# Output projections of a two-layer trunk: tiles 3 to 6 in seven block products per pair

## The chip, the cores and the metric

One core of a Trainium2 chip runs the whole kernel. The time is device microseconds of one launch. The engines are TensorE (PE, with its weight loads as PEld), VectorE (DVE), ScalarE (ACT), GpSimd (POOL) and the queue of SyncE (SP), which here only issues DMAs.

## What is computed

Two layers of a hybrid decoder trunk over 16 learned tokens and 512 others, width 1024, all in float32:

```python
def layer(x):
    h = rmsnorm(x)
    u, z, c_q, c_kv, k_rope, z_mla, g_pool, g_mla = split(h @ w_in)
    y_pool = (pool_mix(u) * silu(z)) @ pool_w_up
    y_mla = (mla(c_q, c_kv, k_rope) * silu(z_mla)) @ mla_w_up      # 8 heads, causal
    merged = sigmoid(g_pool) * y_pool + sigmoid(g_mla) * y_mla
    return x + merged @ w_out                                      # the output projection
```

After the second layer the 16 learned tokens are dropped.

## The kernel before

Everything is held transposed: features on the 128 partitions, tokens along the row (528 in layer 0, 512 in layer 1, where the learned tokens are left out after the keys). A product is made in tiles of 128 output features. Each factor is split into a high and a low part that TensorE multiplies exactly (`whi`, `wlo` of the weights; `hh`, `hl`, `th`, `tl` and so on of the activations), and a product is three matmuls: high by high (L188), high by low (L191), low by high (L192), in `mm3`. ScalarE makes a high part by a copy, VectorE the low part by a subtraction (`split`, `wload`).

The function `stream` runs through a list, `plan`, of products (`Gemm`). Weights come in pieces of 512 columns, four of them ahead, by SP's queue into three buffers `raw`. What happens between two products is written out by hand: `up(name)` runs the stream to a product, `fill_now(ns)` runs it for a while, `after(ns, fn)` puts a job behind it. `behind` makes one instruction wait for another by hand. A scheduler then orders each engine's instructions.

A layer ends with: eight tiles `mu` of the attention's up-projection, whose read-out (`ev_mu`) multiplies by the gate `gms`, adds the pooled half `am` on GpSimd (L1049) and splits the sum into `mg`, that is `hh`/`hl`; and then eight tiles `o` of the output projection. A tile `o` is K = 8 chunks of 128 by the tokens: in layer 0 two halves of 264 columns, so 8 x 3 x 2 = 48 matmuls of 264 columns; in layer 1 24 of 512, its last tile in two halves of 256. Its read-out (`ev_o`, L1063) adds the old residual stream, which SP fetched, and stores the result; in layer 0 it then squares the row for the next norm (`square_x`).

Layer 1 already makes its gate product `gp` in seven block products per pair of tiles (`fast`), a scheme of Strassen and Winograd: weights and activations are cut in two along K, outputs in two along features and tokens, and seven products of sums replace eight. The sums of activations are made by `mixed` in halves; the sums of weights are made in DRAM (`wsum`) by copies on SP's queue and adding DMAs on GpSimd's (`weight_sums`), 32 jobs placed 4500 ns apart over the heads of layer 0. A copy waits by `behind` for a matmul some 9 us back, an add for one some 4 us back.

Of the kernel before, what the change touches and what calls it, by code (L numbers as in the profile page):

```python
# [57 lines left out]
WARM = 8  # L58
SPACE = 4500.0

# [12 lines left out]
def trunk(ctx, tc, xT, pos, win, wkr, wqb, wkb, wvb, wgr, wpu, wmu, wout, gains, const, yT):  # L73
# [88 lines left out]
    class Gemm:  # L162
        def __init__(self, name, src, width, evac=None, xs=None, segs=None, body=None, gain=None):
            self.name, self.src, self.width, self.alloc = name, src, width, mmt
            self.evac, self.xs, self.segs, self.body, self.gain = evac, xs, segs, body, gain
            self.spare = False

# [4 lines left out]

    def wload(src, n, gain, spare):
        raw = early.pop(0) if early else fetch(src, n, rawt(), sp)
# [8 lines left out]
        act.activation(hi[:, :n], raw[:, :n], AF.Copy)  # L183
        dve.tensor_sub(lo[:, :n], raw[:, :n], hi[:, :n].bitcast(F32))  # L184
        return hi, lo
# [13 lines left out]

    newest = [None]  # L200
    plan = []
    done = set()

    def stream():
# [3 lines left out]
        def load(i):  # L208
            g_, c = flat[i]
            n = min(512, g_.width - c)  # L210
            return wload(g_.chunk(c, n), n, g_.gain, g_.spare)

# [116 lines left out]

    wsum = [dp.tile([P, 4, 512], F32, name=f"wsum{u}") for u in range(4)]  # L330
    gate = dp.tile([P, 6, SEQ], F32, name="gate")
# [6 lines left out]

    def weight_sums(w):
        def made(u, i):  # L340
            a, b = w[2 * u], w[2 * u + 1]
            d = wsum[u]
            src = {0: (b[:, 0:512], b[:, 512:1024]), 2: (a[:, 0:512], b[:, 0:512]), 1: (a[:, 0:512], d[:, 0, :]),
                   3: (a[:, 512:1024], d[:, 1, :])}
            return d[:, i, :], src[i]

        def copy(d, src):
            behind(sp.dma_start(d, src[0]), earlier(9000))

        def add(d, src):  # L350
            behind(gp.dma_start(d, src[1], accum_op=ALU.add), earlier(4000))

        for u in range(4):
            for fn, i in ((copy, 0), (copy, 2), (add, 0), (copy, 1), (add, 2), (add, 1), (copy, 3), (add, 3)):
                yield lambda fn=fn, u=u, i=i: fn(*made(u, i))

    class Layer:
        def __init__(self, l):
# [10 lines left out]
            self.csq, self.xsq = [None] * 2, [None] * 8  # L369
            self.sq = []  # L370
            self.f, self.tt, self.part = [None] * 8, [None] * 4, {}
            self.st = self.acc = self.inv = self.cinv = self.kraw = self.kp = None
# [226 lines left out]
        def fast(self, name, a, b, u, got):  # L599
            order = (1, 6, 7, 5, 2, 4, 3)  # L600
            s = wsum[u]
            src = {1: a[:, 0:512], 2: a[:, 512:1024], 4: b[:, 512:1024], 5: s[:, 0, :], 6: s[:, 1, :], 7: s[:, 2, :],
# [439 lines left out]
        def ev_mu(self, m):  # L1042
            def ev(ps, a, b):
                if a == self.x0:
                    self.mg[m] = self.hs[m]
                t = tmp()
                dve.scalar_tensor_tensor(out=t[:, :b - a], in0=self.gms[m][:, a:b], scalar=1.0, in1=ps,  # L1047
                                         op0=ALU.add, op1=ALU.mult)
                gp.tensor_add(t[:, :b - a], t[:, :b - a], self.am[m][:, a:b])  # L1049
                split(*self.mg[m], t[:, :b - a], a, b)  # L1050
            return ev

        def ev_o(self, m, nxt):
            def ev(ps, a, b):
# [17 lines left out]
            return ev  # L1072

        def register(self, nxt):
# [72 lines left out]
        def go(self, nxt):  # L1147
# [11 lines left out]
            if l == 0:  # L1159
                for k in range(8):  # L1160
                    self.square_x(k)
            self.norm_sums()
            up("u1")
            for m in range(2):
# [11 lines left out]
            for s, (a, b) in enumerate(FULL):  # L1176
                a0 = max(a, self.x0)
                self.stat(self.acc[:, a0:b], a0, b, C_CQ, self.acc_last)
            up("qn3")
            self.qk_stats()  # L1180
            if l == 0:
                fill_now(2600)
                for i, fn in enumerate(weight_sums([win[1, MT_GP + m] for m in range(8)])):
                    after(SPACE * (i + 1), fn)
            kq = self.prep(0)
            fill_now(2600)
            due[0] = None
# [22 lines left out]
            if not self.last:  # L1210
                for p in range(4):
                    self.meta_out(p)
            up("o7")
            if nxt is not None:
# [78 lines left out]
```

## Time and profile before

| | |
|---|---|
| median of 3 runs | 788.89 us (788.27 to 788.9) |
| the profiled execution's own time | 788.28 us |
| its span, first to last instruction | 786.4 us |
| mean granted TensorE clock | 1.000 |
| busy: TensorE, VectorE, ScalarE, GpSimd | 778.8, 558.8, 427.1, 210.9 us |
| output projection of layer 0 | 357 to 405 us of the span |
| output projection of layer 1 | 739 to 783 us of the span |

In the profile's rows an operation is named by line, engine, kind and `out<-in`; `xN` is how many it merges, a bracket tells how long the engine was idle before it and who ended that. Matmuls overlap in the records, so TensorE's rate is read from start to start, or from the read-outs of neighbouring tiles.

### The profile page before, as it was taken

What the parts mean: (1) busy time and instruction counts of PE and PEld (TensorE: products, weight loads), DVE (VectorE), ACT (ScalarE), POOL (GpSimd) and SP (SyncE); (2) the same over time, 40 slices, a digit from 0 to 9 for tenths busy, and PEclk for the clock granted to TensorE, in tenths of its full rate; (3) what the DMA queues carried; (4) which work ended last, traced back from release to release, by engine and by line L of the source; (5) the groups of instructions that cost most, each with busy time, mean ns of one, the idle gap of its engine ahead of it and who ended that gap; (6) DMA issues with size and microseconds to landing.
All of it is one profiled execution on the core that took longest, in us unless ns stands there. A gap on an engine that the chain in (4) does not pass through costs nothing.

```text
span 786.4 us, 15094 instructions
## 1 busy us (share of the span) xinstructions
PE 778.8 (99%) x5445; PEld 713.4 (91%) x5445; DVE 558.8 (71%) x1229; ACT 427.1 (54%) x974; POOL 210.9 (27%) x275
## 2 busy tenths in 40 slices
PE   9999999999999999999999999999999999999998
PEld 8999899999999999999997898887778999887887
DVE  5848778447788977685355487775897899874932
ACT  8545655635656665643354455556657676654421
POOL 1034504002434342153000145122004323440600
PEclk9999999999999999999999999999999999999999
DMA  6242343434645435647742422435233454462372
GB/s 243 82 101 84 99 120 102 128 106 117 136 122 126 116 90 112 167 103 176 206 141 81 109 81 79 138 97 167 95 111 112 118 153 126 121 202 68 99 231 100
DMA packets 60907, 97.61 MB, mean 124 GB/s; under 512 B 9744, under 2 KB 18320, under 8 KB 60832
## 3 DMA queue, kind: packets, MB, share of 16 engines
q1 hardware_dynamic: 57520, 90.61, 38.8%
q0 software_dynamic: 2304, 4.20, 4.3%
q10 hardware_dynamic: 1008, 1.84, 0.7%
q8 instruction: 43, 0.70, 0.4%
q14 instruction: 32, 0.26, 0.1%
HBM read 88.64 MB, written 14.23 MB: 131 GB/s over the span
## 4 chain that ended last, share of the span: by engine, by line
PE 91%; DVE 4%; DMA 2%; issue 1%; ACT 1%; ACTq 0%; DVEq 0%
PE mm L188 27%; PE mm L192 27%; PE mm L191 26%; PE mm L944 2%; PE S L191 2%; PE S L192 2%; PE S L188 1%; DVE wlo L184 1%; PE o L950 1%; PE o L949 1%; PE S L498 1%; PE mm L400 1%; DMA xb<-xT 1%; DMA raw<-win 1%; DVE hl L296 0%
## 5 line engine op out<-in xcount | busy, mean ns | idle before, releaser
L188 PE MATMUL mm<-hh,whi 128*128 128x264 f32 (+2 forms) x1080 | 333.9, 311 | 0.1
L191 PE MATMUL mm<-hl,whi 128*128 128x264 f32 (+2 forms) x1080 | 332.5, 309 | 0.4 <-DVE hl L296 0.4
L192 PE MATMUL mm<-hh,wlo 128*128 128x264 f32 (+2 forms) x1080 | 332.1, 310 | 0.4 <-DVE wlo L184 0.4
L184 DVE TENSOR_TENSOR wlo<-raw,whi 128x512 fp32r<-128x512 f32 (+2 forms) x263 | 197.7, 756 | 108.8 <-ACT whi L183 105.3
L183 ACT ACTIVATE whi<-raw 128x512 fp32r<-128x512 f32 (+2 forms) x263 | 157.8, 603 | 179.3 <-PE mm L191 114.6
L188 PEld LDWEIGHTS mm<-hh,whi 128*128 128x128 f32 x1080 | 202.9, 188 | 11.8 <-ACT racc L958 0.5
L191 PEld LDWEIGHTS mm<-hl,whi 128*128 128x128 f32 x1080 | 203.3, 188 | 11.1 <-DVE hl L296 0.9
L192 PEld LDWEIGHTS mm<-hh,wlo 128*128 128x128 f32 x1080 | 202.5, 188 | 10.5 <-DVE wlo L184 1.1
L700 POOL TENSOR_TENSOR racc<-racc,tmp 128x264 f32<-128x264 f32 (+1 forms) x15 | 14.2, 950 | 144.2 <-ACT tmp L699 119.8
L192 PE MATMUL mm<-cq,wlo 128*128 128x264 f32 (+2 forms) x140 | 43.5, 313 | 0.6 <-DVE wlo L184 0.6
L188 PE MATMUL mm<-cq,whi 128*128 128x264 f32 (+2 forms) x140 | 44.0, 314 | 0.0
L191 PE MATMUL mm<-cq,whi 128*128 128x264 f32 (+2 forms) x140 | 43.4, 311 | 0.0
L848 POOL TENSOR_TENSOR tmp<-kp,bc 64x528 f32<-64x528 f32 x16 | 23.7, 1484 | 68.5 <-PE mm L815 44.4
L1049 POOL TENSOR_TENSOR tmp<-tmp,xb 128x264 f32<-128x264 f32 (+1 forms) x24 | 27.2, 1155 | 50.4 <-DVE tmp L1047 38.9
L877 DVE CUSTOM_DVE_ANT_0 S<-S,maskw,nqs 128x288 f32<-128x288 f32 (+4 forms) x80 | 38.3, 497 | 3.0 <-PE S L192 2.8
L922 POOL TENSOR_TENSOR pm<-pa,rs 128x16 f32<-128x16 f32 x32 | 10.9, 340 | 96.7 <-DVE rs L917 88.6
L188 PE MATMUL mm<-u,whi 128*128 128x264 f32 (+1 forms) x108 | 35.2, 326 | 0.1
L296 DVE TENSOR_TENSOR tl<-mm,th 128x512 fp32r<-128x512 f32 (+1 forms) x64 | 29.4, 481 | 7.7 <-ACT th L295 6.5
L192 PE MATMUL mm<-u,wlo 128*128 128x264 f32 (+1 forms) x108 | 34.7, 322 | 0.0
L924 POOL TENSOR_TENSOR cq<-cq,rs 128x384 f32<-128x384 f32 (+1 forms) x32 | 32.8, 1024 | 0.0
L191 PE MATMUL mm<-kn,whi 128*128 128x264 f32 (+1 forms) x96 | 30.6, 320 | 0.0
L188 PE MATMUL mm<-q,whi 128*128 128x264 f32 (+1 forms) x96 | 29.9, 323 | 0.6 <-ACT q L295 0.4
(309 smaller groups left out, 1472.3 us busy)
## 6 DMA issues: line engine op xcount, KB each, us to landing
raw<-win SPq DMA_DIRECT2D x139, 256.0 KB, 2.7
raw<-wout SPq DMA_DIRECT2D x32, 256.0 KB, 3.3
bc<-kdr SPq DMA_DIRECT2D x16, 264.0 KB, 4.1
raw<-wpu SPq DMA_DIRECT2D x16, 256.0 KB, 2.8
wsum<-win SPq DMA_DIRECT2D x16, 256.0 KB, 3.3
raw<-wmu SPq DMA_DIRECT2D x16, 256.0 KB, 2.8
raw<-wsum SPq DMA_DIRECT2D x16, 256.0 KB, 3.2
raw<-wqb SPq DMA_DIRECT2D x12, 256.0 KB, 2.6
```

Source lines behind the costliest of these rows:

```text
L183: act.activation(hi[:, :n], raw[:, :n], AF.Copy)
L184: dve.tensor_sub(lo[:, :n], raw[:, :n], hi[:, :n].bitcast(F32))
L188: first = pe.matmul(out, wh, xh, start=start, stop=False, skip_group_check=more)
L191: pe.matmul(out, wh, xl, start=False, stop=False, skip_group_check=more)
L192: newest[0] = pe.matmul(out, wl, xh, start=False, stop=stop, skip_group_check=more)
L296: dve.tensor_sub(lo[:, a:b], src, hi[:, a:b].bitcast(F32))
L700: self.acc_last = gp.tensor_add(self.acc[:, a:b], self.acc[:, a:b], t[:, :b - a])
L848: gp.tensor_mul(kf[r0:r0 + 64, :], self.kp[r0:r0 + 64, :], bc[r0:r0 + 64, :])
L877: dve.tensor_tensor_reduce(out=sv, in0=sv, in1=mask, scale=nqs[:, i, h:h + 1], scalar=3e38, op0=ALU.add, op1=ALU.min, accum_out=bia[:, c:c ...
L924: gp.tensor_mul(pt[i][:, NM:], pt[i][:, NM:], rs[:, i:i + 1].to_broadcast([P, n - NM]))
L944: pe.transpose(tr[:, P * (i - j):P * (i - j + 1)], pt[i][:, NM + P * j:NM + P * (j + 1)], ident)
L1049: gp.tensor_add(t[:, :b - a], t[:, :b - a], self.am[m][:, a:b])
```

## The change

Of the eight output tiles, 0, 1, 2 and 7 stay as they were. Tiles 3 and 4, and 5 and 6, are made as pairs in seven block products each (`out_pairs`), in both layers: p = 1, 2 and 3 use the activations as they are, p = 4 to 7 the differences that `blend` makes. A product is 4 chunks x 3 = 12 matmuls of half the tokens (264 or 256 columns).

- `blend(k)`, for the four chunk pairs, stands between the `mu` tiles and the first products, while tiles 0 to 2 run: four subtractions on VectorE, in place in `gms`, and three splits. Its first subtraction waits by `behind` for a matmul of the tile in progress.
- `ev_mu` therefore leaves its sum in `gms` in place of a buffer `tmp`.
- Sums of output weights are made in DRAM like those of `gp`: 16 jobs per layer, in the heads. In layer 0 they come first, 3500 ns apart; 22 of the 32 old jobs follow 4000 ns apart, and the other 10 run at the start of layer 1. Layer 1's own 16 are 4500 ns apart in its heads.
- Each product needs its own 512 columns of weights, so weights come for every 12 matmuls of half width. Every second piece uses the slots `kh`/`kl` as raw buffers (`more`).
- The residual rows of tiles 3 to 6 are fetched into `xb` by GpSimd's queue (`residual`), the results are added there and stored by the same queue (`finish`).
- `square_x` of tiles 0 to 6 is made behind the pairs.

```diff
-SPACE = 4500.0
+OUT = (3, 4, 5, 6)
...
+            if g_.more and c % 1024 == 512:
+                return wload(g_.chunk(c, n), n, g_.gain, True, slot(("kh", "kl")[c // 1024 % 2], bufs=2))
...
-                t = tmp()
-                dve.scalar_tensor_tensor(out=t[:, :b - a], in0=self.gms[m][:, a:b], scalar=1.0, in1=ps,
-                                         op0=ALU.add, op1=ALU.mult)
-                gp.tensor_add(t[:, :b - a], t[:, :b - a], self.am[m][:, a:b])
-                split(*self.mg[m], t[:, :b - a], a, b)
+                t = self.gms[m][:, a:b]
+                dve.scalar_tensor_tensor(out=t, in0=t, scalar=1.0, in1=ps, op0=ALU.add, op1=ALU.mult)
+                self.sums[m] = gp.tensor_add(t, t, self.am[m][:, a:b])
+                split(*self.mg[m], t, a, b)
...
-                if b == T:
+                if m == 7:
                     nxt.square_x(m)
...
+        def blend(self, k):
+            a, c = self.x0, T
+            b = (a + c) // 2
+            n = b - a
+            u, w = self.gms[k], self.gms[k + 4]
...
+            behind(dve.tensor_sub(w[:, b:c], u[:, b:c], w[:, b:c]), newest[0])
+            dve.tensor_sub(u[:, b:c], u[:, a:b], u[:, b:c])
+            dve.tensor_sub(u[:, a:b], u[:, a:b], w[:, b:c])
+            dve.tensor_sub(w[:, a:b], w[:, a:b], u[:, a:b])
+            th, tl = slot(f"cq{8 + k}", F32R), slot(f"u{k}", F32R)
+            t3h, t3l, t4h, t4l = (t[:, :n] for t in self.half[4 * k:4 * k + 4])
+            split(th, tl, u[:, a:c], a, c)
+            for h_, l_, v in ((t3h, t3l, w[:, b:c]), (t4h, t4l, w[:, a:b])):
+                split(h_, l_, v, 0, n)
...
+        def residual(self, m):
+            gp.dma_start(xb[:, m, self.x0:T], scr[:, m, :] if self.last else xT[:, m, :])
+
+        def out_pairs(self, nxt):
+            order = [(p, u) for p, u in ((1, 0), (1, 1), (2, 0), (2, 1))] + [(p, u) for u in range(2) for p in (6, 7, 5, 4, 3)]
...
+            def finish(m, s, v):
+                x = xb[:, m, s[0]:s[1]]
+                dve.scalar_tensor_tensor(out=x, in0=v, scalar=0.5, in1=x, op0=ALU.mult, op1=ALU.add)
+                if self.last:
+                    gp.dma_start(yT[:, m, s[0] - NM:s[1] - NM], x)
+                    return
...
+                if p == 1:
+                    act.activation(d, ps, AF.Copy)
+                elif p == 2:
+                    finish(m0, A, ps)
+                elif p == 6:
+                    dve.tensor_sub(d, d, ps)
+                elif p == 7:
+                    dve.tensor_sub(v, ps, d)
+                elif p == 5:
+                    dve.tensor_sub(v, v, ps)
+                    finish(m1, B, v)
...
-            for m in range(8):
+            for m in (0, 1, 2, 7):
+                if m == 7:
+                    self.out_pairs(nxt)
                 add(f"o{m}", wout[l, m], D, evac=self.ev_o(m, nxt), xs=mg,
...
+            if l == 0:
+                jobs.extend(weight_sums("gp", [win[1, MT_GP + m] for m in range(8)]))
+                for i, fn in enumerate(weight_sums(0, [wout[0, m] for m in OUT])):
+                    after(3500 * (i + 1), fn)
+                for i in range(22):
+                    after(16 * 3500 + 4000 * (i + 1), jobs.pop(0))
...
+            if l == 1:
+                for i, fn in enumerate(weight_sums(1, [wout[1, m] for m in OUT])):
+                    after(4500 * (i + 1), fn)
...
+            up("mu7")
+            for m in OUT:
+                self.residual(m)
+            for k in range(4):
+                fill_now(2600)
+                self.blend(k)
             up("o7")
```

How the instructions stand, at the places that matter. First VectorE in layer 0, from the low part of the last gated sum (`hl`) on. Before, only weight splits (L184) and read-outs of tiles (L1063) follow:

```order
L296 TENSOR_TENSOR hl_21_143<-tmp_5205,hh_20_142 128x264
L184 TENSOR_TENSOR wlo_5287<-raw_5284,whi_5286 128x512
L1063 SCALAR_TENSOR_TENSOR xb<-mm_5216,tmp_5261 128x264
L1063 SCALAR_TENSOR_TENSOR xb<-mm_5217,tmp_5277 128x264
L184 TENSOR_TENSOR wlo_5319<-raw_5316,whi_5318 128x512
L184 TENSOR_TENSOR wlo_5360<-raw_5357,whi_5359 128x512
```

Now the four subtractions of `blend` (L1086 to L1089, on the slots `cq`) and the low parts of the differences (L299 into `sq` and `u`) stand among them; read-outs are L1066:

```order
L299 TENSOR_TENSOR hl_21_147<-cq_881_4842,hh_20_146 128x264 x2
L1086 TENSOR_TENSOR cq_825_4512<-cq_734_4040,cq_825_4512 128x264
L184 TENSOR_TENSOR wlo_5324<-raw_5321,whi_5323 128x512
L1087 TENSOR_TENSOR cq_734_4040<-cq_734_4040 128x264
L299 TENSOR_TENSOR sq_5245<-cq_825_4512,sq_5244 128x264
L1088 TENSOR_TENSOR cq_734_4040<-cq_734_4040,cq_825_4512 128x264
L1066 SCALAR_TENSOR_TENSOR xb<-mm_5218,tmp_5289 128x264
L1089 TENSOR_TENSOR cq_825_4512<-cq_825_4512,cq_734_4040 128x264
L1066 SCALAR_TENSOR_TENSOR xb<-mm_5219,tmp_5305 128x264
L1086 TENSOR_TENSOR cq_842_4623<-cq_760_4165,cq_842_4623 128x264
L299 TENSOR_TENSOR u_950_5264<-cq_734_4040,cq_949_5263 128x528
```

From there to the low part of the fourth difference stand 29 operations of 264 columns, 4 of 528 and 6 weight splits.

TensorE in layer 1, where tile 2 before was followed by tile 3 (bank `mm_9911`) in one piece:

```order
L192 MATMUL mm_9870<-hh_20_142,wlo_9867 128x512
L188 MATMUL mm_9911<-hh_6_128,whi_9885 128x512
L191 MATMUL mm_9911<-hl_7_129,whi_9885 128x512
L192 MATMUL mm_9911<-hh_6_128,wlo_9886 128x512
L188 MATMUL mm_9911<-hh_8_130,whi_9885 128x512
```

Now, after tile 2 and the products p = 1 and 2 of the first pair (bank `S_10071`), the first product on a difference (bank `S_10153`, weights `wlo_10130`, difference parts `cq` and `u`) begins, and breaks off after three chunks for the next ones:

```order
L192 MATMUL S_10071<-hh_20_146,wlo_10089 128x256
L192 MATMUL S_10153<-cq_1965_9929,wlo_10130 128x256
L188 MATMUL S_10153<-cq_1972_9970,whi_10129 128x256
L191 MATMUL S_10153<-u_1973_9971,whi_10129 128x256
L192 MATMUL S_10153<-cq_1972_9970,wlo_10130 128x256
L188 MATMUL S_10153<-cq_1982_10017,whi_10129 128x256
L191 MATMUL S_10153<-u_1983_10018,whi_10129 128x256
L192 MATMUL S_10153<-cq_1982_10017,wlo_10130 128x256
L188 MATMUL mm_10173<-sq_9910,whi_10149 128x256
L191 MATMUL mm_10173<-sq_9911,whi_10149 128x256
L188 MATMUL mm_10193<-cq_1965_9929,whi_10169 128x256
```

The widths went from 512 to 256 columns, and each group of 12 matmuls has weights of its own. On VectorE of layer 1, `wlo_10130` has 18 operations of 256 columns and 11 of 512 (itself counted) between it and the last `hl`, and the second pair's first weights, `wlo_10234`, 9 and 6 more.

Last, GpSimd in layer 0. Before, an add of the gated sums is followed by the next, with a job of the weight sums (L351) here and there:

```order
L1049 TENSOR_TENSOR tmp_5120<-tmp_5120,xb 128x264
L1049 TENSOR_TENSOR tmp_5145<-tmp_5145,xb 128x264
L351 DMA wsum_126<-win 128x512
L1049 TENSOR_TENSOR tmp_5163<-tmp_5163,xb 128x264
L1049 TENSOR_TENSOR tmp_5188<-tmp_5188,xb 128x264
```

Now the fetches of residual rows (L1098) stand between the last adds (L1052):

```order
L1052 TENSOR_TENSOR cq_825_4512<-cq_825_4512,xb 128x264
L1098 DMA xb<-xT 128x528
L1052 TENSOR_TENSOR cq_825_4512<-cq_825_4512,xb 128x264
L354 DMA wsumgp_125<-wsumgp_125 128x512
L1098 DMA xb<-xT 128x528
L1052 TENSOR_TENSOR cq_842_4623<-cq_842_4623,xb 128x264 x2
```

Four such fetches stand among the adds of each layer.

More of the change, by code (lines that the diff above doesn't have):

```diff
@@ L165, in __init__ @@
             self.evac, self.xs, self.segs, self.body, self.gain = evac, xs, segs, body, gain
-            self.spare = False
+            self.spare = self.more = False
         def chunk(self, c, n):
@@ L171, in trunk, with wload @@
     loads = [0]
-    def wload(src, n, gain, spare):
-        raw = early.pop(0) if early else fetch(src, n, rawt(), sp)
+    def wload(src, n, gain, spare, buf=None):
+        raw = early.pop(0) if early else fetch(src, n, buf or rawt(), sp)
         loads[0] += 1
@@ L200, in trunk @@
     newest = [None]
+    jobs = []
     plan = []
@@ L328, in trunk @@
     kdr = [dp.tile([H, T], F32, name=f"kdr{l}") for l in range(DEPTH)]
-    wsum = [dp.tile([P, 4, 512], F32, name=f"wsum{u}") for u in range(4)]
+    wsum = {n: [dp.tile([P, 4, 512], F32, name=f"wsum{n}{u}") for u in range(k)] for n, k in (("gp", 4), (0, 2), (1, 2))}
     gate = dp.tile([P, 6, SEQ], F32, name="gate")
@@ L351, in add @@
             behind(gp.dma_start(d, src[1], accum_op=ALU.add), earlier(4000))
-        for u in range(4):
+        for u in range(len(w) // 2):
             for fn, i in ((copy, 0), (copy, 2), (add, 0), (copy, 1), (add, 2), (add, 1), (copy, 3), (add, 3)):
@@ L370, in __init__ @@
             self.sq = []
+            self.sums = [None] * 8
             self.f, self.tt, self.part = [None] * 8, [None] * 4, {}
@@ L1162, in go @@
             self.norm_sums()
+            if l == 1:
+                for i in range(len(jobs)):
+                    after(4000 * (i + 1), jobs.pop(0))
             up("u1")
@@ L1182, in go @@
                 fill_now(2600)
-                for i, fn in enumerate(weight_sums([win[1, MT_GP + m] for m in range(8)])):
-                    after(SPACE * (i + 1), fn)
             kq = self.prep(0)
+            if l == 1:
+                for i, fn in enumerate(weight_sums(1, [wout[1, m] for m in OUT])):
+                    after(4500 * (i + 1), fn)
             fill_now(2600)
@@ L1212, in go @@
                     self.meta_out(p)
+            up("mu7")
+            for m in OUT:
+                self.residual(m)
+            for k in range(4):
+                fill_now(2600)
+                self.blend(k)
             up("o7")
```

56 lines of the change are left out of this document (53 added, 3 removed).

## The prediction

> **What bounds the kernel now.** I read the page first (shares and the chain), then TensorE's waits, then busy time by stretch, and last the timelines of the two output projections.
>
> ```profile
> PE 778.8 (99%) x5445; PEld 713.4 (91%) x5445; DVE 558.8 (71%) x1229; ACT 427.1 (54%) x974; POOL 210.9 (27%) x275
> PE 91%; DVE 4%; DMA 2%; issue 1%; ACT 1%; ACTq 0%; DVEq 0%
> PE wps L137 <- DVE na L817: 1.1, 1, 1.1
> PE mm L192 <- DVE wlo L184: 1.0, 2, 0.6
> 361.50:380.00 18.50, 18.50 (x153) 18.50 (x152) 7.60 (x14) 5.53 (x9) 0.82 (x1) 1.00 0.89 239
> 380.00:405.00 25.00, 25.00 (x206) 25.00 (x205) 11.55 (x21) 11.08 (x19) 0.00 (x0) 1.00 0.59 170
> 747.00:766.00 19.00, 19.00 (x84) 15.43 (x83) 7.63 (x12) 4.42 (x7) 0.00 (x0) 1.00 0.73 233
> 555.00:573.00 18.00, 17.15 (x75) 13.12 (x74) 17.37 (x37) 11.05 (x21) 1.52 (x1) 1.00 0.28 88
> ```
>
> TensorE is busy 99% of the span and 91% of the chain; its longest waits are about 1 us each in total. In the stretches of the output projections (the first three windows; columns: stretch, sum, then busy time and count for PE, PEld, DVE, ACT, POOL, then clock, DMA share, GB/s) it is never idle and its clock is full, while VectorE is busy 7.6 of 18.5 us and 7.6 of 19. So a matmul that is left out there is time saved, as long as its operands come no later. The fourth window is the warning: where VectorE is full (17.37 of 18 us), TensorE loses 0.85 us of 18.
>
> **What goes.** A pair of output tiles is now seven block products instead of eight. VectorE's read-outs of finished tiles give TensorE's rate:
>
> ```profile
> 369.24 0.43 DVE L1063 SCALAR_TENSOR_TENSOR xb<-mm,tmp 128x264 f32<-128x264 f32 x1 [0.46 <-PE mm L192]
> 381.03 0.43 DVE L1063 SCALAR_TENSOR_TENSOR xb<-mm,tmp 128x264 f32<-128x264 f32 x1 [1.06 <-PE mm L192]
> 386.93 0.43 DVE L1063 SCALAR_TENSOR_TENSOR xb<-mm,tmp 128x264 f32<-128x264 f32 x1 [1.06 <-PE mm L192]
> 760.94 0.69 DVE L1063 SCALAR_TENSOR_TENSOR tmp<-mm,tmp 128x512 f32<-128x512 f32 x1 [1.65 <-PE mm L192]
> 766.49 0.69 DVE L1063 SCALAR_TENSOR_TENSOR tmp<-mm,tmp 128x512 f32<-128x512 f32 x1 [1.65 <-PE mm L192]
> 781.84 0.42 DVE L1063 SCALAR_TENSOR_TENSOR tmp<-mm,tmp 128x256 f32<-128x256 f32 x1 [3.57 <-PE mm L192]
> 783.26 0.42 DVE L1063 SCALAR_TENSOR_TENSOR tmp<-mm,tmp 128x256 f32<-128x256 f32 x1 [0.99 <-PE mm L192]
> ```
>
> In layer 0 a tile is 48 matmuls of 264 columns: 386.93 - 381.03 = 5.90 us, 0.1229 us each. A pair goes from 96 to 84, two pairs save 24 x 0.1229 = 2.95 us. In layer 1 a tile is 24 matmuls of 512 columns: 5.55 us, 0.2313 each; the last half of the last tile shows 12 of 256 columns in 1.42 us, 0.1183 each. A pair goes from 48 x 0.2313 = 11.10 to 84 x 0.1183 = 9.94 us, two pairs save 2.32. Together 5.27 us. So a matmul costs about 5.5 ns beyond its columns (2 x 118.3 - 231.3), which layer 1 pays 36 times more per pair. The Trainium skill (TensorE: Matmul & The Clock Gate, "Wait — 56ns, not 53.3ns?") gives columns / 2.4 GHz plus about 2.5 ns, that is 112.5, 215.7 and 109.2 ns; by it the saving would be, as an estimate, 5.06 us instead of 5.27. The rows decide, and they say that the split into halves is dearer and the columns are slower than on that page.
>
> **What is added, and where it lies.** VectorE makes four subtractions and three low parts (one of full width, two of a half) for each of four chunks, between the last low part of the gated sums and the first product that needs a difference. These rows give its rate, by start to start of neighbours:
>
> ```profile
> 353.29 0.42 DVE L296 TENSOR_TENSOR hl<-tmp,hh 128x264 fp32r<-128x264 f32 x1
> 353.63 0.42 DVE L1047 SCALAR_TENSOR_TENSOR tmp<-cq,mm 128x264 f32<-128x264 f32 x1
> 569.37 0.67 DVE L184 TENSOR_TENSOR wlo<-raw,whi 128x512 fp32r<-128x512 f32 x1
> 569.97 0.41 DVE L583 TENSOR_TENSOR cq<-cq,cq 128x256 f32<-128x256 f32 x1
> 570.31 0.41 DVE L584 TENSOR_TENSOR cq<-cq 128x256 f32<-128x256 f32 x1
> 360.98 0.43 DVE L296 TENSOR_TENSOR hl<-tmp,hh 128x264 fp32r<-128x264 f32 x1 [0.20 <-ACT hh L295]
> 746.01 0.68 DVE L296 TENSOR_TENSOR hl<-tmp,hh 128x512 fp32r<-128x512 f32 x1
> ```
>
> 0.34 us for 264 columns (353.29 to 353.63), 0.60 for 512 (569.37 to 569.97), 0.34 for 256 (569.97 to 570.31); 0.62 for 528 is estimated from the slope between them.
>
> *Layer 0.* VectorE's new order has, from the last hl (ends 361.4) to the low part of the fourth difference (u), 29 operations of 264, 4 of 528 and 6 weight splits: 9.9 + 2.5 + 3.6 = 16.0, so 377.4. Tile 1 was read at 369.24, so tile 0 began two tiles earlier, at 357.4; the first product on a difference wants its fourth chunk after 144 + 24 + 9 = 177 matmuls, at 357.4 + 21.8 = 379.2. Slack 1.8 us: cost 0. If the last hl comes 3.4 us late (the third rival) tile 0 itself, which wants it after 40 matmuls (362.3), waits 2.5. Ends 0 and 2.5; I take 0.3, near the lower, since VectorE's row supports it.
>
> *Layer 1.* The last hl ended at 746.7; two weight splits more now stand ahead of it (the ones loaded early into kh and kl), 2 x 0.60: 747.9. Tile 1 ended two tiles before 760.94, at 749.84, so tile 0 began at 738.7 and wants that hl after 40 x 0.2313, at 748.0: no wait. From there to the split of the weights of the first product on a difference (wlo_10130 in the order) stand 18 operations of 256 and 11 of 0.60: 6.1 + 6.6 = 12.7, so 760.6. TensorE wants it after tile 2 and 38 half-wide matmuls: 749.84 + 5.55 + 4.5 = 759.9. It waits 0.7. The next tight place is the second pair's split (wlo_10234): 9 of 256 and 6 of 0.60 more, 3.1 + 3.6, so 767.3, against 749.84 + 5.55 + 88 x 0.1183 = 765.8: 1.5 late in all, and after that a pair of products has 7 x 0.60 + 10 x 0.34 = 7.6 us of VectorE work for 9.9 of TensorE, so the lag shrinks. I take 1.5; ends 0 (VectorE reaches the stage earlier, since sums in place wait for no free tmp) and 3.9.
>
> *Queues.* The residual rows of tiles 3 to 6 are fetched, and their results stored, through GpSimd's queue: four issues among the last adds of each layer.
>
> ```profile
> L351 POOL DMA_DIRECT2D wsum<-win x8 | 6.7, 839 | 56.7 <-PE mm L192 56.7
> L1049 POOL TENSOR_TENSOR tmp<-tmp,xb 128x264 f32<-128x264 f32 x16 | 14.9, 951 | 16.1 <-ACT whi L183 11.5 <-DVE tmp L1047 4.5
> 727.06 4.70 POOL L1049 TENSOR_TENSOR tmp<-tmp,xb 128x512 f32<-128x512 f32 x3 [28.75 <-DVE tmp L1047]
> 729.43 2.88 DVE L184 TENSOR_TENSOR wlo<-raw,whi 128x512 fp32r<-128x512 f32 x2
> 734.26 3.32 POOL L1049 TENSOR_TENSOR tmp<-tmp,xb 128x512 f32<-128x512 f32 x2 [2.49 <-DVE tmp L1047]
> 740.67 4.26 POOL L1049 TENSOR_TENSOR tmp<-tmp,xb 128x512 f32<-128x512 f32 x3 [3.10 <-DVE tmp L1047]
> raw<-wout SPq DMA_DIRECT2D x32, 256.0 KB, 3.3
> wsum<-wsum POOLq DMA_DIRECT2D x8, 256.0 KB, 5.8
> 778.30 5.74 SPq L1067 DMA_DIRECT2D yT<-tmp  x3
> ```
>
> An issue is 0.84 us, four are 3.4. GpSimd idled 4.5 us between its adds in layer 0 and 2.49 + 3.10 = 5.6 in layer 1, waiting for VectorE: that hides them. Each layer's heads get 8 copies on SP's queue and 8 adding DMAs on GpSimd's (5.8 us to landing) for its own output weights; of the 32 old jobs 22 stay in layer 0 and 10 move to the first products of layer 1. SP's loads and GpSimd's window sums and scaling of the probabilities stand behind them. Layer 0 carried 32 such jobs over its heads before with TensorE running on; for layer 1, which had none, no row prices it. Bounds: -0.3 (another order alone) and +1.5 (two landings of 5.8 us of which a quarter shows); I take 0.5. Weights now come every 1.42 us instead of 2.78: 256 KB per 1.42 us is 185 GB/s, under the 239 that the window at 361.5 moved without a wait. The tail is as before: tile 7 stays last, with its two halves and SP's stores; the last GpSimd store is due some 4 us of matmuls earlier.
>
> *Sum*, against the profiled execution's own time (788.28 us; its span is 786.4, so 1.9 lie around it; the median of three runs is 788.89): 788.28 - 5.27 + 0.3 + 1.5 + 0.5 = 785.3. A measurement of this kernel can tell about 0.2%, 1.6 us, from no change.
>
> **Rivals.**
> 1. *All of it arrives.* The sums in place let VectorE run ahead, both layers have slack: 788.28 - 5.27 = 783.0. For it: 7.6 of 19 us busy on VectorE. Against: the 12.7 us counted above leave no slack in layer 1.
> 2. *The gain goes back as small waits.* Each low part needs ScalarE's high part first. If each of the 12 splits of a layer holds VectorE for 0.2 us (the row at 360.98 shows such a 0.20), layer 0 is 2.4 - 1.8 = 0.6 late and layer 1 1.5 + 2.4 = 3.9: 788.28 - 5.27 + 0.6 + 3.9 + 0.5 = 788.0, no change. For it: the window at 555, TensorE losing time where VectorE is full. Against: there only 0.85 us in 18.
> 3. *Slower: GpSimd's queue delays the last sums.* If the four issues don't fall into GpSimd's idle time but push the last adds by 3.4 us, the last hl moves with them, tile 0 waits for it in both layers (2.5 and 3.3), and in layer 1 VectorE's list starts later still behind TensorE's (1.5 as before); differences that then run beside an add slow down, as the two splits at 729.43 did (1.44 us each beside adds, 0.67 alone), 0.5: 788.28 - 5.27 + 2.5 + 3.3 + 1.5 + 0.5 + 0.5 = 791.3, slower. It decides once less than 1 us of the idle is left to fill. For it: the adds are in order behind the issues. Against: GpSimd's idle (4.5, 5.6) was for VectorE, whose products in place now come earlier. The Trainium skill (SBUF — State Buffer, "Who interferes with whom") says that a VectorE operation with two SBUF inputs and a GpSimd operation that reads SBUF block each other for a whole instruction; the trace agrees (1.44 against 0.67).
>
> **How the numbers follow.** Forecast 0.5 (784 to 786.6), rival 1 0.15, rival 2 0.2, rival 3 0.15. Time: 785.3. The range leaves out rival 3 and the very best of rival 1: 783.2 to 788.6. Faster: forecast and rival 1, 0.65; same: rival 2, 0.2; slower: 0.15.
>
> **What would show it.** Right: 48 more matmuls (5493), 84 per pair; read-outs of tiles 0 to 2 still 5.90 and 5.55 apart; the last hl of layer 1 near 748 less what layer 0 gained; TensorE waiting for wlo or u by about 1.5 us in layer 1 and hardly in layer 0. Wrong: waits of TensorE on hl in tile 0 (rival 3); waits of over 3 us in the products (rival 2); a chain that passes through SP's loads there; or heads of layer 1 longer by over 1.5 us.

## The result

The changed kernel took 795.01 us (median of 4 runs, 794.38 to 796.69) against 788.65 before: ratio 1.0084, 95% interval 1.0067 to 1.0102, so 6.4 us slower where 3 us faster was forecast. Its profiled execution took 794.64 us, with a span of 792.8. Three executions among all the runs below took far longer (832.23 us in e5, 934.34 and 1941.56 in e15), and the ratios leave them out.

From the page of the changed kernel, busy time of the engines and the software DMA queue (GpSimd's; packets, MB, share of the DMA engines):

```profile
PE 778.1 (98%) x5493; PEld 713.7 (90%) x5493; DVE 601.0 (76%) x1321; ACT 443.6 (56%) x1015; POOL 238.5 (30%) x315
q0 software_dynamic: 6016, 12.62, 9.8%
```

The same queue before:

```profile
q0 software_dynamic: 2304, 4.20, 4.3%
```

The 48 matmuls more are there (5493). To see what TensorE lost, I took the start of each matmul to the start of the next, less the median of its width (0.122 us for 264 columns, 0.232 for 512, 0.118 for 256), and summed what is over, in us, by stretch of one profiled execution:

| | heads of layer 0 and before (0-355) | its output projection (355-416) | 416-438 | start of layer 1 (438-484) | 484-575 | heads of layer 1 (575-720) | its output projection (720-end) | sum |
|---|---|---|---|---|---|---|---|---|
| before | 17.1 | 0.8 | 1.4 | 1.6 | 4.7 | 6.8 | 0.3 | 32.6 |
| changed | 17.0 | 1.1 | 1.4 | 6.8 | 3.6 | 8.4 | 5.7 | 44.2 |

11.6 us more are lost, 5.27 of matmul time are saved: 6.3, the difference of the two profiled executions (794.64 - 788.28 = 6.36). The loss lies in three places: the start of layer 1 (5.2), layer 1's output projection (5.4), layer 1's heads (1.6); from 484 to 575 us 1.1 less is lost.

**Start of layer 1.** TensorE's waits from 436 to 486 us in the changed kernel (total, times, longest); before it had none there:

```profile
PE mm L188 <- ACT whi L183: 1.4, 1, 1.4
PE mm L188 <- DVE u L545: 1.0, 2, 0.8
PE mm L192 <- DVE wlo L184: 0.7, 2, 0.5
```

The first hangs on a load, as ScalarE's row shows: it stood idle until the weights had landed.

```profile
447.83 1.09 ACT L183 ACTIVATE whi<-raw 128x512 fp32r<-128x512 f32 x2 [6.71 <-DMA raw<-win]
```

The other two stand behind VectorE's work on late data (`wlo`, and the read-out `u`) and weren't traced to their ends. Two windows of the changed kernel (the last two columns are DMA share and GB/s):

```profile
444.00:448.00 4.00, 3.10 (x25) 2.90 (x23) 0.00 (x0) 0.17 (x1) 0.00 (x0) 1.00 1.00 164
448.00:452.00 4.00, 3.27 (x24) 3.06 (x25) 1.88 (x4) 2.68 (x5) 1.77 (x2) 1.00 0.98 231
```

Its loads of the small weights (KB, median us to landing):

```profile
raw<-wkb SPq DMA_DIRECT2D x4, 128.0 KB, 5.7
raw<-wkr SPq DMA_DIRECT2D x1, 128.0 KB, 6.0
```

The same two windows before:

```profile
444.00:448.00 4.00, 4.00 (x23) 3.43 (x22) 0.00 (x0) 0.49 (x2) 1.29 (x1) 1.00 0.65 119
448.00:452.00 4.00, 4.00 (x35) 4.00 (x34) 1.87 (x3) 1.97 (x5) 0.00 (x0) 1.00 0.71 226
```

And the same loads before:

```profile
raw<-wkb SPq DMA_DIRECT2D x4, 128.0 KB, 2.2
raw<-wkr SPq DMA_DIRECT2D x1, 128.0 KB, 2.3
```

The DMA engines are full (1.00 and 0.98, against 0.65 and 0.71) at 164 and 231 GB/s against 119 and 226, and a load of the small weights lands after 5.7 to 6.0 us where 2.2 was enough. GpSimd in the changed kernel shows the second half of it:

```profile
448.08 0.88 POOL L354 DMA_DIRECT2D wsumgp<-wsumgp  x1 [5.52 <-DMA wsumgp<-win]
456.62 0.70 POOL L179 TENSOR_TENSOR raw<-raw,gn 128x256 f32<-128x256 f32 x1 [4.21 <-DMA raw<-wkb]
466.90 0.82 POOL L354 DMA_DIRECT2D wsumgp<-win  x1 [2.38 <-PE mm L192]
```

An adding DMA stands 5.52 us at the head of GpSimd's queue until its copy has landed, another 2.38 us for a matmul; the scaling of the weights (L179) comes at 456.6 where it came at 452.6, although layer 1 began 2.9 us earlier, and what GpSimd owes to the keys behind it is later too.

**Layer 1's output projection.** TensorE's longest wait there in the changed kernel:

```profile
PE mm L191 <- DVE hl L299: 2.0, 1, 2.0
```

VectorE's timeline ahead of it (start, us, what):

```profile
742.96 1.78 DVE L299 TENSOR_TENSOR hl<-cq,hh 128x512 fp32r<-128x512 f32 x1
744.66 0.68 DVE L1051 SCALAR_TENSOR_TENSOR cq<-cq,mm 128x512 f32<-128x512 f32 x1
745.26 0.68 DVE L184 TENSOR_TENSOR wlo<-kh,whi 128x512 fp32r<-128x512 f32 x1
745.87 1.78 DVE L299 TENSOR_TENSOR hl<-cq,hh 128x512 fp32r<-128x512 f32 x1
747.57 0.67 DVE L1051 SCALAR_TENSOR_TENSOR cq<-cq,mm 128x512 f32<-128x512 f32 x1
748.16 0.68 DVE L184 TENSOR_TENSOR wlo<-kl,whi 128x512 fp32r<-128x512 f32 x1
748.77 1.75 DVE L299 TENSOR_TENSOR hl<-cq,hh 128x512 fp32r<-128x512 f32 x1
...
751.04 0.68 DVE L299 TENSOR_TENSOR hl<-cq,hh 128x512 fp32r<-128x512 f32 x1
```

GpSimd's, where the bracket tells the idle time before and what ended it:

```profile
742.52 1.67 POOL L1052 TENSOR_TENSOR cq<-cq,xb 128x512 f32<-128x512 f32 x1 [1.90 <-DVE cq L1051]
744.55 0.56 POOL L1098 DMA_DIRECT2D xb<-scr  x1 [0.36 <-POOL cq L1052]
745.43 1.67 POOL L1052 TENSOR_TENSOR cq<-cq,xb 128x512 f32<-128x512 f32 x1 [0.32 <-DVE cq L1051]
748.32 1.64 POOL L1052 TENSOR_TENSOR cq<-cq,xb 128x512 f32<-128x512 f32 x1 [1.22 <-DVE cq L1051]
```

VectorE is never idle here and goes round in a loop of 2.9 us per tile: product (L1051), a weight split, a low part. Each low part takes 1.78 us in place of 0.68; each of the slow ones lies beside the add that the product just released. Before, the last three products stood in a row. And the order within the loop has changed; the low parts of the sixth and seventh chunk on VectorE, in the order of the program:

```
L299 TENSOR_TENSOR hl_19_145<-cq_1887_9611,hh_18_144 128x512
L1051 SCALAR_TENSOR_TENSOR cq_1907_9681<-cq_1907_9681,mm_9858 128x512
L184 TENSOR_TENSOR wlo_10110<-kl_10107,whi_10109 128x512
L299 TENSOR_TENSOR hl_17_143<-cq_1903_9655,hh_16_142 128x512
```

hl_19 (the seventh chunk) now stands ahead of hl_17 (the sixth), which comes last but one and ends at 750.5. TensorE takes hl_17 first, 28 matmuls behind the start of tile 0 at 741.72, so at 748.2: it waits 2.2 us. What that wait sets off is seen in the windows behind it (PEclk is the last column but two):

```profile
750.50:752.00 1.50, 1.44 (x6) 1.16 (x7) 1.50 (x5) 0.65 (x2) 0.00 (x0) 0.92 0.62 175
752.00:755.00 3.00, 3.00 (x9) 2.33 (x8) 3.00 (x10) 0.97 (x2) 0.00 (x0) 0.50 0.69 201
755.00:757.00 2.00, 2.00 (x10) 1.65 (x9) 1.93 (x5) 1.27 (x3) 0.00 (x0) 0.96 0.03 12
```

For 3.4 us (751.75 to 755.16) the granted clock is 0.50: a 512-column matmul then starts every 0.427 us, not 0.232, and that is 1.6 us more.

### The profile page after: what moved, and what is told of

It reads as the page before. It is cut to its first block, busy times and chain, and to the rows that moved or that the text cites. A ratio compares the mean times of both kernels' runs of the same rounds, so it can differ in the third digit from the quotient of the medians.

```text
span 792.8 us, 15386 instructions
## 1 busy us (share of the span) xinstructions
PE 778.1 (98%) x5493; PEld 713.7 (90%) x5493; DVE 601.0 (76%) x1321; ACT 443.6 (56%) x1015; POOL 238.5 (30%) x315
## 5 line engine op out<-in xcount | busy, mean ns | idle before, releaser
L188 PE MATMUL mm<-hh,whi 128*128 128x264 f32 (+2 forms) x1000 | 308.7, 311 | 2.9 <-ACT whi L183 2.8
L191 PE MATMUL mm<-hl,whi 128*128 128x264 f32 (+2 forms) x1000 | 306.9, 308 | 2.3 <-DVE hl L299 2.3
L192 PE MATMUL mm<-hh,wlo 128*128 128x264 f32 (+2 forms) x1000 | 306.4, 309 | 1.0 <-DVE wlo L184 1.0
L184 DVE TENSOR_TENSOR wlo<-raw,whi 128x512 fp32r<-128x512 f32 (+2 forms) x261 | 195.3, 752 | 100.0 <-ACT whi L183 93.6
L188 PEld LDWEIGHTS mm<-hh,whi 128*128 128x128 f32 x1000 | 188.2, 189 | 14.0 <-ACT whi L183 3.5
L191 PEld LDWEIGHTS mm<-hl,whi 128*128 128x128 f32 x1000 | 188.7, 189 | 12.0 <-DVE hl L299 3.2
L192 PEld LDWEIGHTS mm<-hh,wlo 128*128 128x128 f32 x1000 | 187.8, 189 | 10.4 <-DVE wlo L184 2.1
L1052 POOL TENSOR_TENSOR cq<-cq,xb 128x264 f32<-128x264 f32 (+1 forms) x24 | 28.6, 1220 | 46.8 <-DVE cq L1051 46.6
L299 DVE TENSOR_TENSOR tl<-mm,th 128x512 fp32r<-128x512 f32 (+1 forms) x64 | 29.4, 480 | 7.0 <-ACT th L298 6.0
L354 POOL DMA_DIRECT2D wsum<-wout x8 | 6.8, 848 | 87.8 <-PE mm L192 82.2
L192 PEld LDWEIGHTS mm<-cq,wlo 128*128 128x128 f32 x156 | 29.4, 188 | 2.6 <-DVE wlo L184 1.1
L928 POOL TENSOR_TENSOR cq<-cq,rs 128x384 f32<-128x384 f32 (+1 forms) x32 | 31.6, 989 | 0.0
L888 ACT ACTIVATE cq<-S,bia 128x400 f32<-128x400 f32 (+2 forms) x48 | 24.5, 515 | 12.1 <-DVE bia L916 7.9
```

Source lines behind the costliest of these rows:

```text
L188: first = pe.matmul(out, wh, xh, start=start, stop=False, skip_group_check=more)
L191: pe.matmul(out, wh, xl, start=False, stop=False, skip_group_check=more)
L192: newest[0] = pe.matmul(out, wl, xh, start=False, stop=stop, skip_group_check=more)
L299: dve.tensor_sub(lo[:, a:b], src, hi[:, a:b].bitcast(F32))
L888: act.activation(pv, sv, AF.Exp, scale=-1.0, bias=bia[:, i:i + 1], accum_out=rs[:, c:c + 1])
L928: gp.tensor_mul(pt[i][:, NM:], pt[i][:, NM:], rs[:, i:i + 1].to_broadcast([P, n - NM]))
```

## The experiments

Three theories of the loss were set against the rival on record. A: the ten weight-sum jobs moved to the start of layer 1 delay the weights there (against it stands B: a job costs the same wherever it lies). C: VectorE's order in layer 1 makes tile 0 wait, and the clock drop follows. D (from the second set on): layer 1's own sixteen jobs cost in its heads. The rival is the prediction's third, GpSimd's residual fetches. Every time below stands beside runs of the kernel before on the same chip (788.1 to 788.5), and the ratio is to these; the changed kernel's is 1.0084.

**e1, all 48 jobs in layer 0's heads.**

```diff
-                    after(3500 * (i + 1), fn)
-                for i in range(22):
-                    after(16 * 3500 + 4000 * (i + 1), jobs.pop(0))
+                    after(3000 * (i + 1), fn)
+                for i in range(32):
+                    after(16 * 3000 + 3000 * (i + 1), jobs.pop(0))
```

> All 48 weight-sum jobs of layer 0 run in its heads, 3000 ns apart; none is left for the start of layer 1. Theory A (the ten jobs that were moved to layer 1's first products fill the DMA engines there, and the weight loads land late): the 5 us that TensorE lost between 440 and 483 us go, unless the denser jobs cost something in layer 0's heads: 790 to 791 us against 795.0. Theory B (a job costs the same wherever it lies, by its issue on the queues and its bytes): 795, with the loss moved to 190 to 345 us.

788.22 us, ratio 1.0001 (0.9988 to 1.0014): 6.5 us less than the changed kernel by the ratios, a little more than the 5 expected. The loss from 438 to 484 us fell from 6.8 to 2.4, and the denser jobs cost layer 0's heads nothing (16.4 against 17.0). The output projection of layer 1 kept its 5.6.

**e2, the ten late jobs left out.**

```diff
-            s = wsum["gp"][u]
+            s = wsum["gp"][u % 2]
...
-                for i in range(len(jobs)):
-                    after(4000 * (i + 1), jobs.pop(0))
+                jobs.clear()
```

> The ten late weight-sum jobs are left out altogether (the second half of the gp pairs uses the weights of the first half, so that part of the result is not computed). It prices the ten jobs at the start of layer 1 by themselves. Theory A: 790 us against 795.0, with weight loads from 440 to 483 us landing after some 2.3 us again instead of 5.7 to 6.0. Theory B, or a cause in the pairs of layer 0 that shows only later: 794 to 795.

788.41 us, 1.0007 (0.9999 to 1.0016), with 2.2 lost from 438 to 484. So the ten cost their price by lying at the start of layer 1; in the heads of layer 0 they were free.

**e3, the product in tmp.**

```diff
-                t = self.gms[m][:, a:b]
-                dve.scalar_tensor_tensor(out=t, in0=t, scalar=1.0, in1=ps, op0=ALU.add, op1=ALU.mult)
-                self.sums[m] = gp.tensor_add(t, t, self.am[m][:, a:b])
+                t, v = self.gms[m][:, a:b], tmp()[:, :b - a]
+                dve.scalar_tensor_tensor(out=v, in0=t, scalar=1.0, in1=ps, op0=ALU.add, op1=ALU.mult)
+                self.sums[m] = gp.tensor_add(t, v, self.am[m][:, a:b])
```

> The gated product of the attention's up-projection goes to a buffer tmp again and only the sum is left in gms, which puts VectorE's last products and low parts of layer 1 back into the order of the tiles (hl of tile 5 before that of tile 6). Theory C (sums in place let the scheduler take tile 6 before tile 5 on VectorE; TensorE waits 2.2 us for tile 5's low part in output tile 0, and the clock drop that follows costs 1.6 more): 791 to 792.5 us against 795.0, the wait at 748 us gone or under 1 us. Rival 3 of the prediction (GpSimd's residual fetches among the adds hold the sums): 795, the wait still there.

793.24 us, 1.0060 (1.0044 to 1.0076): 1.9 us less, where 2.5 to 4 were expected. The profile has the mechanism. VectorE:

```profile
743.72 1.27 DVE L1051 SCALAR_TENSOR_TENSOR tmp<-cq,mm 128x512 f32<-128x512 f32 x2
...
747.95 2.51 DVE L299 TENSOR_TENSOR hl<-cq,hh 128x512 fp32r<-128x512 f32 x2
...
750.98 0.68 DVE L299 TENSOR_TENSOR hl<-cq,hh 128x512 fp32r<-128x512 f32 x1
```

Windows over the wait and behind it:

```profile
748.00:751.00 3.00, 2.20 (x10) 1.48 (x9) 3.00 (x5) 1.81 (x4) 1.78 (x2) 1.00 0.90 268
751.00:756.00 5.00, 5.00 (x23) 4.08 (x22) 5.00 (x14) 2.40 (x5) 0.00 (x0) 1.00 0.87 281
```

In the program the order is back (the low part of the sixth chunk before the seventh's), the wait is 0.97 us, the clock stays 1.00, and the stretch loses 2.0 in place of 5.7. That is 3.7 in the execution profiled; the medians show only half of it, and the runs of this kernel lie 5 us apart (790.12 to 795.15).

**e4, the residual fetches behind the last sum.**

```diff
-            gp.dma_start(xb[:, m, self.x0:T], scr[:, m, :] if self.last else xT[:, m, :])
+            behind(gp.dma_start(xb[:, m, self.x0:T], scr[:, m, :] if self.last else xT[:, m, :]), self.sums[7])
```

> The four residual fetches on GpSimd's queue wait for the last gated sum in each layer, so none stands among the adds. Rival 3 of the prediction: the last low parts come up to 3.4 us earlier, the wait at 748 us goes: 790 to 792.5 us against 795.0. Theory C: the adds wait for VectorE's products and not for the fetches (idle before the last two adds ended by the product, 0.3 and 1.2 us), so 794.5 to 795.5.

792.45 us, 1.0063 (1.0048 to 1.0078). The time is what rival 3 expected (790 to 792.5), but the wait that rival 3 explains by the fetches is still there:

```profile
PE mm L191 <- DVE hl L299: 1.8, 1, 1.8
```

So the fetches are not its cause, as the adds' idle time in the changed kernel says (it was ended by VectorE's products, 0.32 and 1.22 us, while an issue takes 0.56). The wait itself gave 0.24 us (1.95 by starts of matmuls, 2.19 in the changed kernel). The profiled execution, the fastest of the six, lost 4.2 in place of 5.7 in layer 1's projection, since its clock stayed at 1.00 behind the wait, 5.4 in place of 6.8 at the start of layer 1 and 0.6 in place of 1.1 in layer 0's projection. Why the last two fell stays open, and the two ratios' intervals overlap (1.0067 and 1.0078).

**e5, both mends (e1 and e3 together).**

> Both mends together: all 48 weight-sum jobs of layer 0 in its heads 3000 ns apart, and the gated product in tmp. If the two losses are separate (weights held back at the start of layer 1; late low parts and a clock drop in layer 1's output projection), they add: 6.8 us off the changed kernel's 795 by the first and 3.6 less by the second, 784 to 785.5 against 788.1 of before, with no wait over 1 us at output tile 0 of layer 1 and the granted clock at 1.00 there. If the second gain of 1.9 us that the median of the run with tmp alone showed is all there is: 786.3.

787.02 us, 0.9983 (0.9968 to 0.9997). By the ratios 8.0 us less than the changed kernel, but 1.5 us over the upper end of what was expected of both gains. The projection of layer 1 lost 1.9, the start 2.2; what stayed is in layer 1's heads: 9.3. Beside e1 the product in tmp is worth 1.4 us, as it was worth 1.9 in e3, and not the 3.7 that left the projection: the heads lost 1.6 more than in e1 (7.7) in the executions profiled, and why stays open.

**e6, and the fetches behind the sums.**

> The same, and the four residual fetches of each layer wait for the last gated sum. If the fetches among the adds cost layer 0 the 0.4 us wait at 361.7 us and layer 1 something like it: 0.5 to 1 us under the run without it. If they cost nothing, the same within 0.5; if they then come too late for the results of the pairs, slower.

788.12 us, 0.9992 (0.9976 to 1.0007): no gain, and with the later fetches layer 1's projection lost 3.8 in the profiled execution where e5 lost 1.9. The fetches among the adds cost nothing here either.

**e7, pairs in layer 0 alone, 48 jobs in its heads.**

```diff
+PAIRS = (0,)
...
-            for m in (0, 1, 2, 7):
-                if m == 7:
+            for m in (0, 1, 2, 7) if l in PAIRS else range(8):
+                if m == 7 and l in PAIRS:
```

> Pairs in layer 0 alone, with all 48 jobs in its heads 3000 ns apart; layer 1 as before the change. By the prediction's term for layer 0 (24 matmuls of 0.1229 us, a wait of 0.3): 785.4 against 788.1 of before. If the crowded heads cost what they save: 788.

783.84 us (783.77 to 784.36), 0.9943 (0.9931 to 0.9955): 4.5 us faster than before, the best of the kernels that compute the whole result, and better than the term. Its output projection:

```profile
361.50:380.00 18.50, 18.50 (x153) 18.50 (x152) 18.28 (x44) 12.32 (x25) 0.00 (x0) 1.00 0.60 171
380.00:405.00 25.00, 25.00 (x207) 25.00 (x206) 19.90 (x38) 14.76 (x25) 4.36 (x8) 1.00 0.48 156
```

VectorE works 18.28 of the first 18.5 us, the low part of the fourth difference ends at 377.65 where 377.4 was counted, and TensorE is never idle. 2.95 of the gain are matmuls; another 1.3 in the execution profiled are smaller losses elsewhere (31.3 in all against 32.6), whose cause wasn't sought.

**e8, pairs in layer 1 alone.**

> Pairs in layer 1 alone; the 32 gp jobs in layer 0's heads 4500 ns apart as before the change, layer 1's own 16 in its heads. By the prediction's terms for layer 1 (2.32 saved, 1.5 waits, part of 0.5): 787.6. By the trace of the changed kernel (5.4 us lost in the output projection, 1.2 in the heads): 791 to 792.5 against 788.1.

795.3 us, 1.0079 (1.0061 to 1.0096): 6.2 us slower, above what was expected. 5.7 are lost in the projection, 9.7 in the heads. The same pairs cost 4.6 us between e7 and e1, and 4.4 between e11 and the changed kernel; the 1.7 us between these and e8 stay open.

**e9, layer 1's sixteen jobs left out (on e5).**

```diff
-                    src[-1] = wsum[l][u][:, {5: 0, 6: 1, 7: 2, 3: 3}[p], :]
+                    src[-1] = wsum[0][u][:, {5: 0, 6: 1, 7: 2, 3: 3}[p], :]
```

> Both mends (48 jobs in layer 0's heads, product in tmp), and layer 1's own 16 weight-sum jobs are left out: the second layer's pairs use the sums of the first layer's output weights, so that part of the result is not computed. It prices layer 1's jobs in its heads. Theory D (they cost about 3 us there: 9.3 us of TensorE's time beyond its pitch from 580 to 720 us with them, 6.0 without): 783.5 to 784.5 against 787.0 with them. If the loss is that of one execution only: 786 to 787.

783.63 us, 0.9939 (0.9920 to 0.9958): the sixteen cost 3.4 us. TensorE's longest wait in layer 1's heads with them (e5):

```profile
PE mm L948 <- POOL pa L928: 1.3, 2, 0.9
```

The window at their start with them:

```profile
575.00:600.00 25.00, 23.71 (x116) 19.41 (x115) 21.97 (x54) 15.25 (x40) 11.32 (x15) 1.00 0.64 149
```

And without them (e9), where TensorE has no such wait:

```profile
575.00:600.00 25.00, 25.00 (x126) 20.99 (x125) 22.06 (x58) 16.86 (x44) 6.35 (x13) 1.00 0.42 125
```

TensorE's wait is for GpSimd's scaling of the probabilities (L928). But GpSimd wasn't held by an adding DMA just before it; in e5 it stood idle until VectorE had the reciprocals (L921):

```profile
591.34 1.12 POOL L926 TENSOR_TENSOR pm<-pa,rs 128x16 f32<-128x16 f32 x1 [2.92 <-DVE rs L921]
```

So the price of the sixteen is shown, and by which step the jobs delay this stage is not; the wait is 1.3 of the 3.4 us.

**e10, all 64 jobs in layer 0's heads, 2250 ns apart (on e3).**

> Product in tmp, and all 64 weight-sum jobs, layer 1's too, in layer 0's heads, 2250 ns apart. If layer 0's heads carry 64 jobs as they carry 48 at no cost: as the run without layer 1's jobs, 783.5 to 784.5. If they are full by then: 786 to 789, with the loss between 190 and 345 us.

792.78 us, 1.0056 (1.0037 to 1.0075). That is above the 786 to 789 expected of full heads. The heads and what stands before them lost 23.0 in place of e9's 16.8: the jobs' tail falls on the last products of layer 0, where ScalarE waited 4.6 us for a weight load (`raw<-wmu`). TensorE's wait there:

```profile
PE mm L188 <- ACT q L298: 3.8, 1, 3.8
```

The window behind it:

```profile
338.00:341.00 3.00, 3.00 (x15) 3.00 (x15) 2.43 (x8) 1.45 (x5) 0.00 (x0) 0.50 0.98 183
```

One wait of 3.8 us, and again half the clock behind it.

**e11, e7 with the change's placement of the jobs.**

> Pairs in layer 0 alone (783.84 with all 48 jobs in the heads), with the change's own placement of the jobs: 16 at 3500 ns, 22 at 4000 ns, and ten at the start of layer 1. It prices the ten late jobs by themselves, without layer 1's pairs. Theory A: 5 to 6.5 us more, 789 to 790.5, so that the gain of layer 0 is gone by them alone. Theory B: 784 to 785.

790.62 us, 1.0028 (1.0018 to 1.0038): the ten late jobs cost 6.8 us by themselves (6.7 by the ratios), more than the 5.27 that both layers' pairs save in matmuls. 6.2 were lost from 438 to 484, 4.0 more than in e7; the rest is spread in small pieces.

**e12, layer 1's jobs 8500 ns apart (on e5).**

> Both mends, with layer 1's own 16 jobs 8500 ns apart in place of 4500, so over nearly all of its heads. If it is their density that costs: 785 to 786 against 787.0. If each job costs what it costs: 787 as before; if the last sums then come too late for the pairs: 788 or more, with a wait of the weight loads at 760 us.

787.49 us, 0.9992 (0.9979 to 1.0006): no gain. In the execution profiled the heads lost 7.4 in place of e5's 9.3, but the jobs end later, and the projection lost 3.1 in place of 1.9: there the weights of a pair came late, and TensorE waited once more (1.08 us at 763.6). From 484 to 575 us 1.1 more was lost. So wider spacing doesn't pay as a whole; whether the density is part of the price isn't settled.

**e13 and e14, the late copies alone and the late adds alone (on e11).**

```diff
-                for i in range(len(jobs)):
-                    after(4000 * (i + 1), jobs.pop(0))
+                for i, fn in enumerate(jobs):
+                    if i in (0, 2, 3, 5, 8):
+                        after(4000 * (i + 1), fn)
```

> Pairs in layer 0 alone with ten late jobs (790.62) stripped to the five copies on SP's queue; the five adding DMAs are left out (so five of the sums of gp weights are not completed). With none of the ten the time was 783.84. If the copies do it, by lying among the weight loads on SP's queue and sharing the DMA engines with them: 788 or more. If GpSimd's adds do it, by holding up its queue: 784 to 785.5.

> The other half: the five copies move to layer 0's heads (27 jobs there, 3200 ns apart), the five adding DMAs stay at the start of layer 1, 8000 ns apart. If GpSimd's adds do it: 788 or more. If the copies do it: 784 to 785.5. If each does its share by the DMA engines' time: about 787 in both.

786.63 (0.9981, 0.9971 to 0.9991) and 786.24 us (0.9972, 0.9962 to 0.9981), so 3.0 and 2.3 us over e7 by the ratios: each half has its share, and together they cost more (6.7) than the two apart (5.3). The small weights of that stage landed after 3.1 and 3.6 us, against 2.0 in e7 and 7.2 in e11.

**e15, layer 1's sixteen jobs ahead of its heads (on e5).**

> Both mends, and layer 1's own 16 jobs 4000 ns apart from about 485 to 550 us, behind its kr products and ahead of its heads, where VectorE and GpSimd are less busy (GpSimd 9.5 of 72 us from 484 to 556). If it is the heads that make them dear: 783.5 to 784.5, as with layer 1's jobs left out (783.63), against 787.0. If each job costs what it costs anywhere in layer 1: 787.

0.9958 (0.9943 to 0.9973), about 785.1 us by the ratio and 2.0 under e5, between the two expectations; its heads lost 5.9 in place of 9.3, in a profiled execution that was the fastest of its runs (782.91). The sixteen still cost 1.5 us beside e9, less than in the heads, and the kernel isn't better than pairs in layer 0 alone.

## Why the prediction was wrong

- *Matmul time, -5.27.* Right in both layers. Layer 1's first sums of squares came at 418.9 in place of 421.8 us, 2.9 for the 2.95 forecast, and the balance above closes with 5.27. (One figure beside it was off: 2 x 118.3 - 231.3 is 5.3 ns, not 5.5; the sum doesn't use it.)
- *Layer 0's wait, 0.3.* Right: one wait of 0.4 at 361.7 on hl, none on the differences; with the denser jobs (e7) it is gone. It was near: the low part of the fourth difference ended at 378.85, 1.4 of the 1.8 us of slack later than counted.
- *Weight-sum jobs, 0.5, bounded by -0.3 and 1.5.* The step that failed most. Its upper bound was not even its own working: a quarter of two landings of 5.8 us is 2.9, and 1.5 is a quarter of one. With 2.9 it would still have been too low, for it priced ten jobs at the start of layer 1 as if they were in layer 0's heads, where 32 had run with TensorE going on. The ten cost 6.8 us (e11), the sixteen in layer 1's heads 3.4 (e9). "No row prices it" was true of the jobs, but the rows of the place were there: loads of 2.2 us to landing, a DMA share of 0.65 to 0.71 before anything was added, and L179 waiting 7.2 us for its load. In the heads of layer 0 all 48 jobs were free (e1); at the start of layer 1 ten weren't.
- *Layer 1's waits, 1.5, ends 0 and 3.9.* 5.4, over the upper end. The place was missed: among the products stood one wait of 0.49 us; hl in tile 0 was the large one. The prediction asked when the last hl is ready and when it is wanted (after 40 matmuls, which the program still has), and took the order of the others as it was; the sixth was the late one. VectorE's content was undercounted too: low parts beside adds take 1.78 us. The product in place, which the prediction counted only as a help, is what turned the order: with the product in tmp (e3) the wait is 0.97. Of the 5.4, 2.2 are the wait, 1.6 the clock behind it, the rest small pieces.
- *Rival 3* named the right place in layer 1, an amount near it (3.3), and the slowing of VectorE beside an add, but GpSimd's fetches as the cause; e4 and e6 speak against these. Its layer 0 half (2.5) was wrong, its 791.3 still 3.7 short.
- *What would show it wrong* did: TensorE waited on hl in tile 0, and layer 1's heads lost 1.6 us more, just over the bound named.

## To carry to other kernels

Price a DMA that is moved by the place where it lands: how long loads take there, how full the DMA engines are, and how far ahead the weights are fetched; that it was free in another stage says nothing. When an operation's buffer changes (in place, or another pool), compare the order of every producer with the order in which TensorE takes the results, not the last of them alone. Where TensorE loses some 2 us within one 3.41 us window of its clock (below), up to 1.6 us more can go through the clock.

## What was not expected of the hardware

The granted clock fell after waits that are short, and the traces show when. In all 17 kernels the changes of the clock lie whole windows of 3.41 us behind its first rise, and each drop before the end lasts one window: in the changed kernel the clock rose at 4.23 us and fell at 751.75, 219 windows later, until 755.16. What decides is the time that TensorE loses within one such window (by starts of matmuls, as in the table). Six kernels had a drop, and the window ahead of it had lost 2.1 to 2.3 us, in e10 all of its 3.4. No other window between the first rise and the last matmul, in any kernel, lost more than 1.91, and none was followed by a drop.

So the length of a wait doesn't decide alone. At 446.8 us two kernels waited alike. In e13 the wait of 1.54 us and a smaller one behind it fell into one window, which lost 2.1:

```profile
446.80:450.21 3.41, 1.81 (x13) 1.39 (x12) 1.69 (x3) 1.52 (x4) 0.00 (x0) 1.00 0.40 143
450.21:453.62 3.41, 3.41 (x18) 3.41 (x17) 1.08 (x3) 1.32 (x3) 0.00 (x0) 0.50 0.69 221
```

In the changed kernel a window ended in the middle of the wait of 1.56 us, and the two lost 1.05 and 1.15:

```profile
444.55:447.96 3.41, 2.56 (x21) 2.35 (x19) 0.00 (x0) 0.13 (x1) 0.00 (x0) 1.00 0.98 156
447.96:451.37 3.41, 2.63 (x19) 2.43 (x20) 1.78 (x3) 2.23 (x5) 1.14 (x2) 1.00 0.98 241
```

The wait of 1.95 us in e4 was cut in the same way, with 1.6 lost in the fuller window; the wait of 2.19 us in four kernels fell into one window each time. The Trainium skill (TensorE: Matmul & The Clock Gate, "What's actually happening") has the clock halved after an idle window of about 3.4 us, and says that the windows run freely, whatever the kernel does. The windows here agree with it; that 2.1 us of idle time in one is enough differs from that page, and the measurement decides.

The DMA engines were reported full (share 1.00) at 164 GB/s while a copy within DRAM ran beside the loads on SP's queue (GpSimd's queue moved nothing from 444 to 448 us), where 239 GB/s came with a share of 0.89 in layer 0's projection before. The Trainium skill (DMA: Bandwidth & Descriptors, "Queues, rings and completion order") says that each DMA engine serves its queues in turn, packet by packet; the small weights' landing, 2.0 us in e7 and 3.6 with the adds of GpSimd's queue alone beside them (e14), agrees with it. The share of time, not GB/s, is what told here whether there was room.
